# Down of a feed-forward: three of eight quads (two of six at the end) as seven products, with the weight sums by a load and an accumulating load

## The chip, the core and the metric

The kernel runs on one core of a Trainium2 chip. The metric is the device time of one execution in microseconds (us); shown is the median of three runs. TensorE (PE in the profile) multiplies, VectorE (DVE) and ScalarE (ACT) work element by element, GpSimd (POOL) does a little arithmetic and issues some DMAs, SyncE (SP) issues the loads of the weights.

## The reference

Two layers of a streaming encoder over 256 tokens of width 2048, all in float32. Layer 0 has a gated and pooled mixer, layer 1 a latent attention; each is followed by a feed-forward with 5632 hidden channels, where the change is:

```python
def swiglu(h, w_gate, w_up, w_down):
    return (jax.nn.silu(h @ w_gate) * (h @ w_up)) @ w_down
...
        x = x + mix
        x = x + swiglu(rmsnorm(x, g_ffn[layer]), w_gate[layer], w_up[layer], w_down[layer])
```

## The kernel before

Every float32 product is made of three faster ones: both factors are split into a high part (fp32r) and the rest, and TensorE multiplies high by high, high by rest, rest by high (`token_product`, lines 211 to 213, one matmul of 128x512 each). Activations are split once. Weights are split as they arrive: ScalarE copies the high part (wh, line 105), VectorE subtracts it (wl, line 106). There are six buffers of 1024 columns for each of wh and wl.

The feed-forward (`feed_forward`) goes through the hidden channels in three parts of 4, 4 and 3 groups of 512. A part first makes its hidden channels (gate and up, one call of `quads` per group), and then multiplies them by their rows of w_down, which adds to the trunk x ("Down"). Down of a part of four is two blocks, each one call of `quads` with eight quads for two blocks of 512 output columns; Down of the last part is one block of six quads, and its other 1024 output columns follow as plain token-major products with w_e.

A quad is a square of two by two tiles: two token halves, two k tiles of activations (x11, x21, x12, x22), two k tiles times two column blocks of weights (b11, b12, b21, b22; one load of 1 MB). Done plainly it is eight products, which add to the four PSUM banks c11, c12, c21, c22. Those are the four buffers of the pool ps_mm ("mm" in the profile), and the next call of `quads` gets the same four banks in the same order. In some quads the eight products are made as seven, from sums of activations and sums of weights (`quad_seven`, `quads`); four of these products add to p1, p6, p5, p7, the four banks of ps_sm ("sm"), which are combined with c once the last such quad is through. In Down `between` does that: after the last quad of seven ScalarE copies p6, and eight VectorE instructions add p1, p5, p7 and the copy to x. After the whole block four more VectorE adds bring c11, c21, c12, c22 to x (`evict`, line 316, recorded at line 253). Only then can the next call of `quads` write to these banks.

Which quads are made as seven is set by hand: `SEVEN` for gate and up, `SEVEN_DOWN` for Down, there by the number of groups in the part. The sums of activations that quads of seven need are made in `split_pair` when the hidden channels are transposed, and kept in `hforms`.

Two of the four sums of weights, t1 = b11 + b12 and t3 = b12 + b22, are one add over 1024 columns. Either VectorE adds them (`quad_seven` without t13, into the tile sums), or the loads do: GpSimd loads 1024 columns to a tile t13 (two buffers; "t" in the profile) and then a second time with an accumulating DMA (`sums_of`, lines 573 and 574). The second load waits for the first to land. Before, only the gate/up quads in `SUMMED` use loads.

The order on each engine is that of the recorded program after a scheduler has moved instructions; engines wait for each other by semaphores, each goes through its own row in order. The weights of up to three quads are asked for ahead (`AHEAD`), as far as buffers allow.

Of the kernel before, what the change touches and what calls it, by code (L numbers as in the profile page):

```python
# [8 lines left out]
F32 = mybir.dt.float32  # L9
F32R = mybir.dt.float32r  # L10
AF = mybir.ActivationFunctionType
ALU = mybir.AluOpType
AX = mybir.AxisListType

P = 128
# [7 lines left out]
SEVEN = (3, 5, 6, 7)  # L23
SUMMED = (3, 6, 7)

SEVEN_DOWN = {4: (3, 5), 3: (3,)}
AHEAD = 2
EPS = 1e-6
NH = 16
# [6 lines left out]
def trunk(ctx: ExitStack, tc: tile.TileContext, a: dict, out: bass.AP):  # L36
    nc = tc.nc
# [11 lines left out]
    def stage(**bufs):  # L49

        st = ExitStack()
        return st, *(st.enter_context(tc.tile_pool(name=n, bufs=b)) for n, b in bufs.items())

    def ev(shape, dtype=F32):

        return evs.tile([P, *shape], dtype, name="ev")
# [11 lines left out]
    at = 0  # L68
# [30 lines left out]
    def split_raw(raw, n, step=SPLIT):  # L99
        parts = []  # L100
        for o in range(0, n, step):
            m = min(step, n - o)
            wh = whs.tile([P, SPLIT], F32R, name="wh")
            wl = wls.tile([P, SPLIT], F32R, name="wl")
            nc.scalar.activation(out=wh[:, :m], in_=raw[:, o:o + m], func=AF.Copy)  # L105
            nc.vector.tensor_tensor(out=wl[:, :m], in0=raw[:, o:o + m], in1=wh[:, :m].bitcast(F32), op=ALU.subtract)  # L106
            parts.append((wh, wl, m))
        return parts
# [271 lines left out]
    def hidden():  # L380
        return big.tile([P, KD, 2 * T], F32R, name="hid")
# [8 lines left out]
    def token_sums():  # L390
        return stat.tile([P, 2, 4], F32, name="tsum")
# [8 lines left out]
    for k0 in range(0, KD, 2):  # L400
        raw = raws.tile([P, 2 * SPLIT], F32, name="raw")
        if k0 <= 2:

            n = 512 if k0 == 0 else 1024
# [52 lines left out]
    st, att, qpool = stage(att=1, qpool=2)  # L457
# [46 lines left out]
    for m in range(8):  # L504
# [10 lines left out]
        u = ev([T])  # L515
# [5 lines left out]
        for t in range(2):  # L521
            nc.vector.scalar_tensor_tensor(out=y[:, t * P:(t + 1) * P], in0=mix[:, t * P:(t + 1) * P], scalar=gain("v", m),
                                           in1=wb[:, 1, :], op0=ALU.mult, op1=ALU.add)
# [26 lines left out]
    def quad_eight(raw):  # L550
        parts = split_raw(raw, 2048)
        return dict(zip(("b11", "b12", "b22", "b21"), (block(parts, i) for i in range(4))))

    def chunks_of(layer, early):

        wgu, wd, we = (a[f"{n}{layer}"] for n in ("w_gu", "w_d", "w_e"))
        quad = lambda j, seven: "seven" if j in seven else "eight"
        todo = []
        at = 0
        for n in PARTS:  # L560
            for c in range(at, at + n):
                todo += [(wgu[c, j], "summed" if j in SUMMED else quad(j, SEVEN)) for j in range(KD // 2)]
            last = at + n == sum(PARTS)
            for b in range(1 if last else 2):
                todo += [(wd[b, 2 * at + j], quad(j, SEVEN_DOWN[n])) for j in range(2 * n)]
            if last:
                todo += [(we[c, :, i * 512:(i + 4) * 512], "whole") for c in range(2) for i in range(0, 4 * n, 4)]
            at += n

        def sums_of(src):  # L570

            t13 = early.tile([P, 1024], F32, name="t13")
            nc.gpsimd.dma_start(out=t13, in_=src[:, :1024])  # L573
            nc.gpsimd.dma_start(out=t13, in_=src[:, 512:1536], accum_op=ALU.add)
            return t13

        def load(src, kind, t13):
            raw = raws.tile([P, 2 * SPLIT], F32, name="raw")
            nc.sync.dma_start(out=raw, in_=src)
            if kind == "whole":  # L580
                return split_raw(raw, 2 * SPLIT)
            return quad_eight(raw) if kind == "eight" else quad_seven(raw, t13)

        count, begun, ready = len(todo), [], []
        for n in range(count):
            while len(ready) <= AHEAD and (todo or begun):
                while todo and len(begun) < 3:
                    src, kind = todo.pop(0)
                    begun.append((src, kind, sums_of(src) if kind == "summed" else None))
                ready.append(load(*begun.pop(0)))  # L590
            yield ready.pop(0)
# [45 lines left out]
    def feed_forward(layer, sums, scaled, g_next):  # L637
        f = None
        after = token_sums()
        at = 0  # L640
        st, hds, early = stage(hds=2, early=2)
        chunks = chunks_of(layer, early)
        for part, n in enumerate(PARTS):
            hid = hidden()
            seven_d = SEVEN_DOWN[n]
            final = part == len(PARTS) - 1

            hforms = hds.tile([P, 2, 2, 3, P] if not final else [P, 1, 2, 4, P], F32R, name="hforms", bufs=1)
            for c in range(n):
                e22 = []  # L650
                cs, (p1, p6, p5, p7) = quads(KD // 2, SEVEN, xs, scaled["forms"], chunks,
                                             lambda j, cs, ps: e22.append(copy(cs[3])) if j == KD // 2 - 2 else None)
                if f is None:
                    f = stat.tile([P, 2], F32, name="factor")
                    nc.vector.tensor_tensor(out=f, in0=trunk_rstd(sums), in1=scaled["back"], op=ALU.mult)
                e22, = e22
                e11, e12, e21, u2 = *(copy(p) for p in cs[:3]), copy(p6)
                add(e11, p1, e11)
                add(u2, p1, u2)
                add(e12, p5, e12)  # L660
                sub(e12, e12, u2)
                add(u2, p7, u2)
                add(e21, u2, e21)
                add(e22, p5, e22)
                sub(e22, e22, u2)
                hd = []
                for t, (g, u) in enumerate(((e11, e12), (e21, e22))):
                    nc.scalar.activation(out=g, in_=g, func=AF.Silu, scale=f[:, t:t + 1])
                    h = hds.tile([P, 512], F32, name="hd")
                    nc.vector.scalar_tensor_tensor(out=h, in0=u, scalar=f[:, t:t + 1], in1=g, op0=ALU.mult, op1=ALU.mult)  # L670
                    hd.append(h)
                for m in (0, 2):
                    def put(pt, hid=hid, hforms=hforms, seven_d=seven_d, m=4 * c + m):
                        pair = hid[:, m:m + 2, :]
                        src = pt.rearrange("p (j t) -> p j t", j=2)
                        if m // 2 in seven_d:
                            hg = ev([2, T])
                            nc.scalar.activation(out=hg, in_=src, func=AF.Copy)
                            split_pair(pair, hg, hforms[:, seven_d.index(m // 2)])
                        else:  # L680
                            split_pair(pair, src)
                    pending.append(lambda m=m, hd=hd, put=put: turned(lambda t, j: hd[t][:, (m + j) * P:(m + j + 1) * P], put))

            def pair_into(c, evict, hid=hid, hforms=hforms, seven_d=seven_d):
                s0, s1 = slice(c * 512, (c + 1) * 512), slice((c + 1) * 512, (c + 2) * 512)

                def between(j, cs, ps):
                    if j != seven_d[-1]:
                        return
                    if final and g_next == "final":  # L690
                        nonlocal gfin
                        gfin = big.tile([P, D], F32, name="sums")
                        nc.scalar.dma_start(out=gfin, in_=a["g_final"].broadcast_to([P, D]))
                    p1, p6, p5, p7 = ps
                    u2 = copy(p6)
                    add(x[:, 0, s0], p1, x[:, 0, s0])
                    add(u2, p1, u2)
                    add(x[:, 0, s1], p5, x[:, 0, s1])
                    sub(x[:, 0, s1], x[:, 0, s1], u2)
                    add(u2, p7, u2)  # L700
                    add(x[:, 1, s0], x[:, 1, s0], u2)
                    add(x[:, 1, s1], p5, x[:, 1, s1])
                    sub(x[:, 1, s1], x[:, 1, s1], u2)

                (c11, c12, c21, c22), _ = quads(2 * n, seven_d, hid, hforms, chunks, between)
                evict(c, (c11, c21))
                evict(c + 1, (c12, c22))

            into_trunk(None, 0, 4 * n, hid, g_next if final else None, after, chunks, pairs=range(1 if final else 2), pair_into=pair_into)
            at += n  # L710
        st.close()
        return after

    sums = feed_forward(0, sums, scaled, "mix1")

    def rotated(s):
# [12 lines left out]
    st, att, qpool = stage(att=1, qpool=2)  # L729
# [22 lines left out]
    u, y = rotated(s)  # L752
# [73 lines left out]
    for p in range(10):  # L826
# [4 lines left out]
        for i in range(3):  # L831
            if p < 8:
# [3 lines left out]
                else:  # L836
                    s = ev([T])
                    nc.vector.tensor_tensor(out=s, in0=ps, in1=rqs, op=ALU.mult)
                    u, y = rotated(s)
# [108 lines left out]
```

## Time and profile before

| | us |
|---|---|
| median of three runs (1904.33 to 1907.59) | 1904.38 |
| the profiled execution | 1904.91 |
| its span, first to last instruction | 1903.1 |
| busy: TensorE, VectorE, ScalarE, GpSimd | 1890.4, 1584.0, 1149.7, 103.9 |
| mean granted clock of TensorE, share of full speed | 0.999 |

A matmul is shown from its own start to its modelled end, and the next one starts before that; the pace is read from the starts. An instruction's time is shown with an idle time before it and what ended this idle time, where there was one.

### The profile page before, as it was taken

What the parts mean: (1) busy time and instruction counts of PE and PEld (TensorE: products, weight loads), DVE (VectorE), ACT (ScalarE), POOL (GpSimd) and SP (SyncE); (2) the same over time, 40 slices, a digit from 0 to 9 for tenths busy, and PEclk for the clock granted to TensorE, in tenths of its full rate; (3) what the DMA queues carried; (4) which work ended last, traced back from release to release, by engine and by line L of the source; (5) the groups of instructions that cost most, each with busy time, mean ns of one, the idle gap of its engine ahead of it and who ended that gap; (6) DMA issues with size and microseconds to landing.
All of it is one profiled execution on the core that took longest, in us unless ns stands there. A gap on an engine that the chain in (4) does not pass through costs nothing. (4 is left out here: it accounts for less than half of the span.)

```text
span 1903.1 us, 24047 instructions
## 1 busy us (share of the span) xinstructions
PE 1890.4 (99%) x8994; PEld 1586.9 (83%) x8994; DVE 1584.0 (83%) x2067; ACT 1149.7 (60%) x1538; POOL 103.9 (5%) x159
## 2 busy tenths in 40 slices
PE   9999999999999999999999999999999999999998
PEld 8888888888888888888889988888888888888886
DVE  7785589998799987999675755899987999978995
ACT  6554676664567654666555755776655667546663
POOL 0000001000011100000000000000100011001000
PEclk9999999999999999999999999999999999999999
DMA  8567568885688865786455255588866888757863
GB/s 310 200 219 240 183 209 291 274 266 208 215 275 274 293 235 192 251 277 237 177 180 182 93 173 194 191 278 285 262 223 208 261 289 269 255 201 254 264 238 127
DMA packets 74277, 440.19 MB, mean 231 GB/s; under 512 B 8496, under 2 KB 10288, under 8 KB 30256
## 3 DMA queue, kind: packets, MB, share of 16 engines
q1 hardware_dynamic: 53136, 364.93, 52.8%
q0 software_dynamic: 19008, 69.21, 15.4%
q10 hardware_dynamic: 2016, 4.51, 0.7%
q8 instruction: 70, 1.15, 0.2%
q14 instruction: 47, 0.39, 0.1%
HBM read 436.52 MB, written 2.10 MB: 230 GB/s over the span
## 5 line engine op out<-in xcount | busy, mean ns | idle before, releaser
L105 ACT ACTIVATE wh<-raw 128x1024 fp32r<-128x1024 f32 (+1 forms) x692 | 669.6, 986 | 470.2 <-PE mm L213 312.3
L106 DVE TENSOR_TENSOR wl<-raw,wh 128x1024 fp32r<-128x1024 f32 (+1 forms) x692 | 772.4, 1133 | 165.8 <-ACT wh L105 163.6
L211 PE MATMUL mm<-wh,xs 128*128 128x512 f32 x880 | 344.0, 391 | 0.7 <-ACT ev L252 0.7
L212 PE MATMUL mm<-wl,xs 128*128 128x512 f32 x880 | 342.5, 389 | 0.0
L213 PE MATMUL mm<-wh,xs 128*128 128x512 f32 x880 | 342.2, 389 | 0.0
L211 PE MATMUL mm<-wh,hid 128*128 128x512 f32 x852 | 333.3, 391 | 0.4 <-ACT ev L252 0.3
L213 PE MATMUL mm<-wh,hid 128*128 128x512 f32 x852 | 332.0, 390 | 0.0
L212 PE MATMUL mm<-wl,hid 128*128 128x512 f32 x852 | 331.7, 389 | 0.0
L105 ACT ACTIVATE wh<-sums 128x1024 fp32r<-128x1024 f32 x146 | 154.8, 1060 | 102.1 <-DVE sums L253 58.4
L106 DVE TENSOR_TENSOR wl<-sums,wh 128x1024 fp32r<-128x1024 f32 x146 | 177.8, 1221 | 28.6 <-ACT wh L105 24.8
L211 PEld LDWEIGHTS mm<-wh,xs 128*128 128x128 f32 x880 | 165.2, 188 | 35.0 <-ACT ev L252 1.2
L213 PEld LDWEIGHTS mm<-wh,xs 128*128 128x128 f32 x880 | 165.2, 188 | 34.3
L212 PEld LDWEIGHTS mm<-wl,xs 128*128 128x128 f32 x880 | 165.3, 188 | 33.6
L211 PEld LDWEIGHTS mm<-wh,hid 128*128 128x128 f32 x852 | 160.0, 188 | 33.7 <-ACT ev L252 0.8
L213 PEld LDWEIGHTS mm<-wh,hid 128*128 128x128 f32 x852 | 160.0, 188 | 33.2
L212 PEld LDWEIGHTS mm<-wl,hid 128*128 128x128 f32 x852 | 160.1, 188 | 32.5
L135 PE MATMUL mm<-xs,wh 128*128 128x512 f32 x375 | 133.8, 399 | 0.0
L106 DVE TENSOR_TENSOR wl<-t,wh 128x1024 fp32r<-128x1024 f32 x66 | 80.6, 1222 | 36.2 <-ACT wh L105 36.2
L136 PE MATMUL mm<-xs,wl 128*128 128x256 f32 x375 | 104.8, 280 | 0.0
L105 ACT ACTIVATE wh<-t 128x1024 fp32r<-128x1024 f32 x66 | 70.0, 1060 | 35.6 <-PE mm L213 29.8
L253 DVE TENSOR_TENSOR ev<-sm,ev 128x512 f32<-128x512 f32 x130 | 83.4, 682 | 2.4 <-ACT ev L252 2.4
L573 POOL DMA_DIRECT2D t<-in_w_gu x66 | 38.9, 590 | 835.2 <-DVE wl L106 718.0
(237 smaller groups left out, 2649.4 us busy)
## 6 DMA issues: line engine op xcount, KB each, us to landing
raw<-in_w_gu SPq DMA_DIRECT2D x176, 1024.0 KB, 5.9
raw<-in_w_d SPq DMA_DIRECT2D x76, 1024.0 KB, 4.9
t<-in_w_gu POOLq DMA_DIRECT2D x132, 512.0 KB, 6.8
raw<-in_w_o SPq DMA_DIRECT2D x32, 1024.0 KB, 4.9
raw<-in_w_e SPq DMA_DIRECT2D x12, 1024.0 KB, 4.9
raw<-in_w_v SPq DMA_DIRECT2D x10, 1024.0 KB, 6.6
raw<-in_w_z SPq DMA_DIRECT2D x8, 1024.0 KB, 4.9
raw<-in_w_u SPq DMA_DIRECT2D x8, 1024.0 KB, 4.9
```

The lines of the kernel that those rows point to most:

```text
L105: nc.scalar.activation(out=wh[:, :m], in_=raw[:, o:o + m], func=AF.Copy)
L106: nc.vector.tensor_tensor(out=wl[:, :m], in0=raw[:, o:o + m], in1=wh[:, :m].bitcast(F32), op=ALU.subtract)
L135: nc.tensor.matmul(ps, lhsT=wh, rhs=mv, start=first, stop=False)
L136: nc.tensor.matmul(ps[:, :T], lhsT=wl, rhs=mv[:, :T], start=False, stop=last)
L211: nc.tensor.matmul(ps, lhsT=hi, rhs=wh, start=first, stop=False)
L212: nc.tensor.matmul(ps, lhsT=hi, rhs=wl, start=False, stop=False)
L213: nc.tensor.matmul(ps, lhsT=lo, rhs=wh, start=False, stop=last)
L253: add = lambda out, p, q: nc.vector.tensor_tensor(out=out, in0=p, in1=q, op=ALU.add)
L573: nc.gpsimd.dma_start(out=t13, in_=src[:, :1024])
```

## The change

Quads of seven in Down: 3, 5 and 6 of eight instead of 3 and 5, and 3 and 4 of six instead of 3. All of them now take t1 and t3 from `sums_of`. `hforms` grows, and the product of gate and up is written over the up half, instead of to a tile of its own.

```diff
-SEVEN_DOWN = {4: (3, 5), 3: (3,)}
+SEVEN_DOWN = {4: (3, 5, 6), 3: (3, 4)}
...
-                todo += [(wd[b, 2 * at + j], quad(j, SEVEN_DOWN[n])) for j in range(2 * n)]
+                todo += [(wd[b, 2 * at + j], "summed" if j in SEVEN_DOWN[n] else "eight") for j in range(2 * n)]
...
-        st, hds, early = stage(hds=2, early=2)
+        st, hds, early = stage(hds=1, early=2)
...
-            hforms = hds.tile([P, 2, 2, 3, P] if not final else [P, 1, 2, 4, P], F32R, name="hforms", bufs=1)
+            hforms = hds.tile([P, len(seven_d), 2, 4 if final else 3, P], F32R, name="hforms")
...
-                    h = hds.tile([P, 512], F32, name="hd")
-                    nc.vector.scalar_tensor_tensor(out=h, in0=u, scalar=f[:, t:t + 1], in1=g, op0=ALU.mult, op1=ALU.mult)
-                    hd.append(h)
+                    nc.vector.scalar_tensor_tensor(out=u, in0=u, scalar=f[:, t:t + 1], in1=g, op0=ALU.mult, op1=ALU.mult)
+                    hd.append(u)
```

What moves on the engines is seen in their rows. First VectorE at the end of the first Down block of layer 0, from the middle of the eight instructions of `between` on (sm_3884 is p7; mm_3727, 3729, 3728, 3730 are c11, c21, c12, c22 of this block; wl are splits of the weights of the quads to come). Before, where `between` belongs to quad 5:

```order
L254 TENSOR_TENSOR x_82<-x_82,ev_3971 128x512
L106 TENSOR_TENSOR wl_3984<-raw_3981,wh_3983 128x1024
L253 TENSOR_TENSOR ev_3971<-sm_3884,ev_3971 128x512
L106 TENSOR_TENSOR wl_3988<-raw_3981,wh_3987 128x1024
L253 TENSOR_TENSOR x_82<-x_82,ev_3971 128x512
L254 TENSOR_TENSOR x_82<-x_82,ev_3971 128x512
L106 TENSOR_TENSOR wl_4018<-raw_4015,wh_4017 128x1024
L106 TENSOR_TENSOR wl_4022<-raw_4015,wh_4021 128x1024
L253 TENSOR_TENSOR x_82<-mm_3727,x_82 128x512
L253 TENSOR_TENSOR x_82<-mm_3729,x_82 128x512
L253 TENSOR_TENSOR x_82<-mm_3728,x_82 128x512
L253 TENSOR_TENSOR x_82<-mm_3730,x_82 128x512
```

And in the changed kernel, where `between` belongs to quad 6 (sm_3892 is p7; mm_3722, 3724, 3723, 3725 are c11, c21, c12, c22):

```order
L254 TENSOR_TENSOR x_82<-x_82,ev_4021 128x512
L106 TENSOR_TENSOR wl_4037<-raw_4034,wh_4036 128x1024
L253 TENSOR_TENSOR ev_4021<-sm_3892,ev_4021 128x512
L106 TENSOR_TENSOR wl_4041<-raw_4034,wh_4040 128x1024
L253 TENSOR_TENSOR x_82<-x_82,ev_4021 128x512
L254 TENSOR_TENSOR x_82<-x_82,ev_4021 128x512
L253 TENSOR_TENSOR x_82<-mm_3722,x_82 128x512
L253 TENSOR_TENSOR x_82<-mm_3724,x_82 128x512
L253 TENSOR_TENSOR x_82<-mm_3723,x_82 128x512
L253 TENSOR_TENSOR x_82<-mm_3725,x_82 128x512
L106 TENSOR_TENSOR wl_4079<-raw_4076,wh_4078 128x1024
L106 TENSOR_TENSOR wl_4083<-raw_4076,wh_4082 128x1024
```

The eight instructions of `between` come one quad later, and the two splits that stood between them and the four adds of c now stand behind these adds. The ends of the eight blocks of parts of four and of the last part's block in layer 0 read like this, nine in all.

Second, GpSimd from the last gate/up quad of the first part on. Before, the loads of the next part's gate/up quads follow:

```order
L573 DMA t13_3504<-in_w_gu0 128x1024
L574 DMA t13_3504<-in_w_gu0 128x1024
L573 DMA t13_4327<-in_w_gu0 128x1024
L574 DMA t13_4327<-in_w_gu0 128x1024
L573 DMA t13_4453<-in_w_gu0 128x1024
```

In the changed kernel the loads for six Down quads (3, 5, 6 of both blocks) stand between, here down to the second block's first:

```order
L573 DMA t13_3498<-in_w_gu0 128x1024
L574 DMA t13_3498<-in_w_gu0 128x1024
L573 DMA t13_3668<-in_w_d0 128x1024
L574 DMA t13_3668<-in_w_d0 128x1024
L573 DMA t13_3760<-in_w_d0 128x1024
L574 DMA t13_3760<-in_w_d0 128x1024
L573 DMA t13_3831<-in_w_d0 128x1024
L574 DMA t13_3831<-in_w_d0 128x1024
L573 DMA t13_4031<-in_w_d0 128x1024
L574 DMA t13_4031<-in_w_d0 128x1024
```

With two buffers, quad 6's tile (t13_3831) is the one that quad 3's (t13_3668) leaves free.

Third, VectorE at the end of the last part's Down block in layer 1, where each eviction is followed by a multiplication by the final gain (line 324). Before, from the middle of `between` on (mm_15925, 15927, 15926 are c11, c21, c12):

```order
L254 TENSOR_TENSOR x_82<-x_82,ev_16094 128x512
L106 TENSOR_TENSOR wl_16107<-raw_16104,wh_16106 128x1024
L253 TENSOR_TENSOR ev_16094<-sm_16070,ev_16094 128x512
L106 TENSOR_TENSOR wl_16111<-raw_16104,wh_16110 128x1024
L253 TENSOR_TENSOR x_82<-x_82,ev_16094 128x512
L254 TENSOR_TENSOR x_82<-x_82,ev_16094 128x512
L106 TENSOR_TENSOR wl_16141<-raw_16138,wh_16140 128x1024
L106 TENSOR_TENSOR wl_16145<-raw_16138,wh_16144 128x1024
L253 TENSOR_TENSOR x_82<-mm_15925,x_82 128x512
L253 TENSOR_TENSOR x_82<-mm_15927,x_82 128x512
L253 TENSOR_TENSOR x_82<-mm_15926,x_82 128x512
```

In the changed kernel (mm_16062, 16064, 16063 are c11, c21, c12; two splits and the first steps of `between` stand ahead of these rows):

```order
L253 TENSOR_TENSOR ev_16284<-sm_16226,ev_16284 128x512
L106 TENSOR_TENSOR wl_16297<-raw_16294,wh_16296 128x1024
L254 TENSOR_TENSOR x_82<-x_82,ev_16284 128x512
L106 TENSOR_TENSOR wl_16301<-raw_16294,wh_16300 128x1024
L253 TENSOR_TENSOR ev_16284<-sm_16229,ev_16284 128x512
L253 TENSOR_TENSOR x_82<-mm_16062,x_82 128x512
L253 TENSOR_TENSOR x_82<-x_82,ev_16284 128x512
L254 TENSOR_TENSOR x_82<-x_82,ev_16284 128x512
L253 TENSOR_TENSOR x_82<-mm_16064,x_82 128x512
L324 TENSOR_TENSOR x_82<-x_82,sums_16282 128x512
L253 TENSOR_TENSOR x_82<-mm_16063,x_82 128x512
```

Here c11's add stands ahead of the last two instructions of `between`, and a multiplication by the gain ahead of c12's.

## Rows read from the trace of the kernel before

**Rows 1.** Busy time of TensorE on the page: us, share of the span, instructions.

```profile
PE 1890.4 (99%) x8994; PEld 1586.9 (83%) x8994; DVE 1584.0 (83%) x2067; ACT 1149.7 (60%) x1538; POOL 103.9 (5%) x159
```

**Rows 2.** Waits of TensorE, the longest: us in total, times, longest.

```profile
PE mm L211 <- ACT ev L252: 1.1, 2, 0.7
```

**Rows 3.** Windows: PE, PEld, DVE, ACT, POOL busy; clock, DMA share, GB/s.

```profile
408.23:451.28 43.05, 43.05 (x195) 35.74 (x194) 40.86 (x50) 23.72 (x28) 0.85 (x1) 1.00 0.74 252
451.28:493.40 42.12, 42.12 (x187) 34.90 (x186) 34.52 (x39) 20.49 (x22) 0.00 (x0) 1.00 0.56 200
366.50:408.23 41.73, 41.73 (x189) 34.61 (x188) 40.24 (x51) 28.14 (x36) 4.22 (x6) 1.00 0.88 278
```

**Rows 4.** Timeline of TensorE, quad 5's end and the next block's start: start, duration.

```profile
440.18 0.39 PE L213 MATMUL sm<-wh,hforms 128*128 128x512 f32 x1
440.40 0.39 PE L211 MATMUL mm<-wh,hid 128*128 128x512 f32 x1
...
451.28 0.39 PE L211 MATMUL mm<-wh,hid 128*128 128x512 f32 x1
...
451.96 0.39 PE L211 MATMUL mm<-wh,hid 128*128 128x512 f32 x1
```

**Rows 5.** Timeline of VectorE in the same stretch.

```profile
438.14 0.68 DVE L253 TENSOR_TENSOR x<-sm,x 128x512 f32<-128x512 f32 x1
438.74 2.35 DVE L106 TENSOR_TENSOR wl<-raw,wh 128x1024 fp32r<-128x1024 f32 x2
441.01 0.68 DVE L253 TENSOR_TENSOR x<-sm,x 128x512 f32<-128x512 f32 x1
441.61 0.68 DVE L253 TENSOR_TENSOR ev<-sm,ev 128x512 f32<-128x512 f32 x1
...
446.87 0.69 DVE L254 TENSOR_TENSOR x<-x,ev 128x512 f32<-128x512 f32 x1
447.48 2.35 DVE L106 TENSOR_TENSOR wl<-raw,wh 128x1024 fp32r<-128x1024 f32 x2
449.75 2.48 DVE L253 TENSOR_TENSOR x<-mm,x 128x512 f32<-128x512 f32 x4
```

**Rows 6.** Timeline of ScalarE, the copy of p6.

```profile
440.60 0.60 ACT L252 ACTIVATE ev<-sm 128x512 f32<-128x512 f32 x1 [0.29 <-PE sm L213]
```

**Rows 7.** Timeline, layer 1, end of the last Down block: VectorE and TensorE.

```profile
1860.95 1.88 DVE L253 TENSOR_TENSOR x<-mm,x 128x512 f32<-128x512 f32 x3
...
1861.29 0.39 PE L213 MATMUL mm<-wh,hid 128*128 128x512 f32 x1
...
1861.78 0.47 PE L211 MATMUL mm<-wh,hid 128*128 128x512 f32 x1
...
1862.09 0.39 PE L212 MATMUL mm<-wl,hid 128*128 128x512 f32 x1
```

**Rows 8.** Timeline, the same block: VectorE behind p1 and p5; quad 3's end.

```profile
1849.40 3.49 DVE L106 TENSOR_TENSOR wl<-raw,wh 128x1024 fp32r<-128x1024 f32 x3
...
1850.63 0.39 PE L211 MATMUL mm<-wh,hid 128*128 128x512 f32 x1
```

**Rows 9.** Groups by line and shape: busy us, mean ns of one, idle before.

```profile
L253 DVE TENSOR_TENSOR sums<-raw 128x1024 f32<-128x1024 f32 x40 | 48.9, 1222 | 3.9 <-DMA raw<-in_w_gu 3.6
...
L275 DVE TENSOR_TENSOR ev<-ev 128x128 f32<-128x128 f32 x18 | 5.1, 286 | 0.1
```

**Rows 10.** Timeline of GpSimd: the loads that meet the pair before them.

```profile
403.39 0.87 POOL L573 DMA_DIRECT2D t<-in_w_gu  x1
414.08 0.85 POOL L574 DMA_DIRECT2D t<-in_w_gu  x1 [9.82 <-DMA t<-in_w_gu]
```

**Rows 11.** Lines 573 and 574, from issue to landing.

```profile
DMA to landing us min/median/max: 3.9/5.8/11.6
...
DMA to landing us min/median/max: 5.4/7.6/13.1
```

**Rows 12.** Timeline of VectorE, first Down block: quad 3's sums.

```profile
417.25 1.22 DVE L253 TENSOR_TENSOR sums<-raw 128x1024 f32<-128x1024 f32 x1
...
421.32 1.22 DVE L106 TENSOR_TENSOR wl<-sums,wh 128x1024 fp32r<-128x1024 f32 x1
```

## Prediction

> **What bounds the kernel now.** I read the busy shares first: TensorE is busy for 99% of the span [rows 1]. A busy share alone doesn't prove a bound, so the next view is TensorE's list of waits: its longest entry adds up to 1.1 us over the whole run [rows 2]. Then the windows: one from the start of a part's first Down block to its end, the second block, and the gate/up column group ahead of them. TensorE has no idle time in any of the three, at a granted clock of 1.00 (2.4 GHz), while VectorE is busy for 40.9 of 43.1 us, 34.5 of 42.1 and 40.2 of 41.7, and the DMA share is highest, 0.88, in gate/up [rows 3]. So TensorE sets the pace, and VectorE is close behind. Last the timeline, for the pace itself: one matmul of 512 columns starts 0.226 us after the one before, although it is shown with 0.39 us [rows 4]; over the 48 matmuls of the two quads from 440.40 to 451.28 it is 10.88 / 48 = 0.2267 us [rows 4]. I use 0.2267. Three matmuls (one product) take 0.68 us, a quad of eight products 24 x 0.2267 = 5.44 us, one of seven 4.76 us.
>
> **What is removed from TensorE.** Each layer runs two Down blocks in each of two parts of four and one in the part of three, so five blocks, and each gets one more quad of seven. That is 10 quads, each three matmuls shorter: 30 x 0.2267 = 6.8 us. Nothing else of TensorE's work changes.
> The row says 0.2267 us for one such matmul. The Trainium skill, "TensorE: Matmul & The Clock Gate", section "Back-to-back issue gap", gives about 131 ns for 512 columns in a sustained stream; by that the 30 matmuls would be an estimated 3.9 us, and my end result 2.9 us higher. The row doesn't agree with it, and the row decides.
>
> **What moves between VectorE and the loads.** A quad that now has its two sums loaded loses the add of 1024 columns, 1.22 us [rows 9]. A quad that becomes one of seven gains three things on VectorE: 1536 more columns to split (a split of 1024 at 1.22 us [rows 12], one of 512 at the 0.68 us of the 512-column adds in [rows 5]) and two adds of 512 (0.68 each). Per block of eight quads: minus 2 x 1.22, plus 1.22 + 0.68 + 2 x 0.68 = 3.26, so 0.8 us more. The first block of a part also makes one more set of sums of the activations: four subtractions of 128 columns at 0.286 us [rows 9] and a split of 384 columns, below 0.68 us; ScalarE gets two more copies, each at most the 0.60 us of a 512-column one [rows 6]. On this total VectorE stays below TensorE: 34.5 + 0.8 of 41.4 us in a second block; in a first one the durations add up to 40.9 + 2.6 = 43.5 of 42.4, but neighbours overlap (they start 0.60 us apart at a duration of 0.68 [rows 5]), over the 50 instructions [rows 3] by 4 us. I cost this at nothing: the cover is the three quads of lead that the splits have. Without cover the price is at most those 0.8 to 2.6 us a block. The product that was written to a tile of its own and is now written over the up half has the same size, and costs nothing.
>
> **What is moved to the end of the block: the term that decides.** The four ps_sm sums p1, p6, p5, p7 can be taken out only when the last quad of seven is through. Before, that is quad 5, with quads 6 and 7 behind it (10.88 us); now it is quad 6, with only quad 7 behind it (5.44 us). I call E the moment at which the last quad of seven ends on TensorE. In the block shown E = 440.40 and the next block begins at 451.28 [rows 4]. ScalarE copies p6 at E + 0.20 to E + 0.80 [rows 6]. VectorE, without idle time, takes p1, makes two splits, is at p5 at E + 0.61 and at the last of the eight instructions at 446.87; at 447.48, E + 7.08, it is through with them [rows 5]. Two more splits follow, then the four adds that empty c11, c21, c12, c22, from 449.75, 0.60 us apart [rows 5]. The first, c11's, ends at 449.75 + 0.68 = 450.43, which is 0.85 us ahead of 451.28, where the next block's first product writes the same bank. The third, c12's, ends at 451.63, 0.33 us ahead of 451.96, where c12's bank is written again [rows 4]. So it fits today, with little to spare.
> In the changed order VectorE's row from E on is the same up to the last of the eight (the splits in between are those of the next two quads, as before), and the four adds follow at once. Then c11's add starts at E + 7.08 and ends at E + 7.76, and c12's ends at E + 8.96. The next block is due at E + 5.44, and c12's product at E + 6.12. c11 is 2.32 us late, c12 2.84 us. How TensorE starts again is seen once in the rows: the add that begins at 1860.95 frees c11's bank at 1861.63, the matmul starts at 1861.78, 0.15 us later, and the one after it 0.31 us behind, 0.08 more than the usual pace [rows 7]. So c12's product starts at E + 9.11 instead of E + 6.12, 2.99 us late, and 0.08 is lost in starting: **3.07 us a block end**. c21 and c22 are out in time by then. Queued behind TensorE's wait is all the rest of the kernel, and nobody gives the time back, since TensorE is never behind on anything else.
> Nine of the ten block ends have this order (in layer 0 the last one leads into the plain token-major blocks, which use c11's and c12's banks in the same turn). The tenth is the end of layer 1. There E is 1850.63, and VectorE was through with p1 and p5 at 1849.40, E - 1.23 [rows 8]. Two splits at 1.14 us (two take 2.27 us in [rows 5]) bring it to E + 1.04; in the new order six steps (0.60, 1.14, 0.60, 1.14, 0.60 and then c11) put c11's add at E + 5.12, and after four more of 0.60 before it c12's starts at E + 8.12 and ends at 8.80. With 0.15 and 0.08, against 6.12, that is 2.9 us; the block end loses 1861.78 - 1861.52 + 0.08 = 0.34 us already [rows 7], so 2.6 are new.
> Bounds for this price, from both sides: if all four splits were done before E, VectorE would start at E + 0.80 with p6's copy, and seven adds of 0.60 and c11's 0.68 end at E + 5.68, c12's at 6.88, so that c12 is 0.99 us late with its start: 1.0 us a block end at least, as the eight instructions themselves don't fit into 5.44 us. Upwards it grows by whatever VectorE is late at E; I take 3.07, since the splits stand between in the order and the rows show them there.
>
> **The sum.** Profiled execution 1904.9; - 6.8 + 9 x 3.07 + 2.6 = + 23.4, so 1928.3; the median shown is 0.5 us lower than the profiled run: **1927.8 us**, 1.2% slower. Less than 0.2% (3.8 us) can hardly be told from no change here.
>
> **Rivals.**
> 1. The sums come out in time and the gain stays: 1904.4 - 6.8 = 1897.6, faster. It needs c11's bank free within 5.44 us of E, that is, four splits and one of the eight instructions moved out of the way. For it speaks that the evictions fit today; against it that the margin is 0.85 us, while quad 6's 5.44 us go and only two splits (2.27 us) are taken out from between. Chance 0.05.
> 2. The block ends cost less, 1.0 to 2.2 us, because VectorE has some of the splits behind it: 1904.4 - 6.8 + 10 to 22 = 1908 to 1920. Chance 0.08, of which 0.04 end within 0.2% of before.
> 3. The loads of quad 6's sums come late on top. There are two buffers for them, so quad 6's first load waits for quad 3's split. In the first block that split begins at 421.32 today and one add (1.13 us) earlier after the change, so it ends at 421.4 [rows 12]. First load 5.8 us, 0.3 to the next issue, accumulating load 7.6 (medians) [rows 11]: 435.1. VectorE needs them at 438.0, because two adds of 0.60 and a split of 1.22 must be done at 440.40, when quad 6 begins. With a load that meets other traffic, as the pair from 403.39, issued again at 414.08 [rows 10] and landed 7.6 later, it is 439.7: 1.7 us late. In four first blocks that is 7 us: 1935. With the longest of each, 11.6 and 13.1 [rows 11], it would be 8.4 us a block. Chance 0.12.
>
> The forecast itself has the remaining 0.75, with 1921 to 1933 as its own range (0.7 us either way at each block end). The range given reaches from rival 2's upper part to rival 3: 1917 to 1937. Slower by over 0.2%: 0.75 + 0.12 + 0.04 = 0.91; within: 0.04; faster: 0.05.
>
> **What the profile after would show.** Right: ten gaps of TensorE in Down, at each block's end, some 2.4 us before the first product and some 0.5 before the second, each ended by a VectorE add of x from an mm bank; 30 fewer matmuls at the old pace; no gap elsewhere. Wrong: the four adds early enough and no gap (rival 1), shorter gaps with splits ahead of p1 (rival 2), or a gap in front of quad 6 of a first block, with VectorE waiting for a load (rival 3). What would make all of this wrong is a VectorE that, at the last quad of seven, runs further ahead or further behind than in [rows 5].

## The result and the profile after

The changed kernel takes 1951.31 us (median of four runs, 1943.11 to 1963.08) against 1904.68 us before (four runs, 1904.33 to 1907.59): a ratio of 1.0244, interval 1.0223 to 1.0265. The forecast was 1927.8 with a range of 1917 to 1937. The direction was right; the loss is twice the forecast one. The profiled execution is the longest of the four, with a span of 1961.3 us against 1903.1.

The page first: busy times, then TensorE's granted clock in 40 slices (one 8 where all were 9).

```profile
PE 1906.1 (97%) x8964; PEld 1594.0 (81%) x8964; DVE 1603.5 (82%) x2119; ACT 1168.1 (60%) x1570; POOL 142.9 (7%) x215
...
PEclk9999999998999999999999999999999999999999
```

Against [rows 1] there are the 30 matmuls fewer that were expected, yet TensorE is busy for longer. Its list of waits (us in total, times, longest), where [rows 2] had 1.1 us at the top:

```profile
PE mm L211 <- DVE x L253: 31.1, 9, 5.9
PE mm L212 <- DVE wl L106: 9.0, 3, 3.7
PE mm L211 <- ACT wh L105: 2.3, 1, 2.3
```

The first and third lines are the block ends; the second is a wait that the forecast's sum did not contain (its rival 3 did). Windows: the first Down block up to the restart behind it, the second one in the same way (both had no idle time in [rows 3]), and two stretches behind a wait. Columns as in [rows 3].

```profile
408.23:460.23 52.00, 44.49 (x193) 36.12 (x192) 42.27 (x56) 27.59 (x33) 5.06 (x7) 0.94 0.86 272
460.23:506.25 46.02, 43.73 (x183) 35.73 (x184) 35.66 (x41) 21.99 (x23) 4.20 (x6) 0.95 0.74 239
442.96:447.40 4.44, 4.44 (x12) 3.49 (x13) 4.44 (x5) 3.88 (x4) 0.55 (x1) 0.62 0.85 172
460.79:465.50 4.71, 4.71 (x15) 3.70 (x14) 3.35 (x4) 0.27 (x1) 0.00 (x0) 0.61 0.48 165
```

So there are three losses, and the rows below take them one by one. A wait is counted from start to start of two matmuls, less the pace of 0.2267 us.

**The end of a second block** is as forecast, less one step. TensorE, then VectorE (start, duration, in brackets idle time and what ended it):

```profile
503.57 0.39 PE L213 MATMUL mm<-wh,hid 128*128 128x512 f32 x1
506.25 0.47 PE L211 MATMUL mm<-wh,xs 128*128 128x512 f32 x1 [2.30 <-ACT wh L105]
...
507.02 0.40 PE L211 MATMUL mm<-wh,xs 128*128 128x512 f32 x1
...
499.56 0.68 DVE L253 TENSOR_TENSOR ev<-sm,ev 128x512 f32<-128x512 f32 x1
...
504.83 0.68 DVE L254 TENSOR_TENSOR x<-x,ev 128x512 f32<-128x512 f32 x1
505.43 2.47 DVE L253 TENSOR_TENSOR x<-mm,x 128x512 f32<-128x512 f32 x4
```

Quad 6 ended at 498.36 (E). The four adds begin at 505.43, E + 7.07, where E + 7.08 was forecast; the first ends at 506.11, and TensorE restarts at 506.25, 0.14 later. The wait is 506.25 - 503.57 - 0.23 = 2.45 us. The bracket names ScalarE, but the splits of this quad's weights, which come after that copy, were through by 504.30; the add of 505.43 is what came 0.14 ahead. Then the second bank is written at 507.02, while the third add runs to 507.31: the matmul did not wait for it, only for the first two (the second ends at 506.71). The banks that the changed program assigns say why: behind these blocks the next c12 lies in the bank that c21 had, and the next c21 in that of c12. All four second blocks show 2.46 us.

**In front of quad 6 of a first block** a load is late. GpSimd, VectorE and TensorE:

```profile
422.55 0.55 POOL L573 DMA_DIRECT2D t<-in_w_d  x1 [6.67 <-DVE ev L274]
429.82 0.85 POOL L574 DMA_DIRECT2D t<-in_w_d  x1 [6.72 <-DMA t<-in_w_d]
...
421.03 1.22 DVE L106 TENSOR_TENSOR wl<-t,wh 128x1024 fp32r<-128x1024 f32 x1
...
440.35 0.69 DVE L253 TENSOR_TENSOR sums<-t,raw 128x512 f32<-128x512 f32 x1 [7.00 <-issue]
...
440.48 0.39 PE L211 MATMUL mm<-wh,hid 128*128 128x512 f32 x1
442.96 0.50 PE L212 MATMUL mm<-wl,hid 128*128 128x512 f32 x1 [2.09 <-DVE wl L106]
```

Quad 3's split of its t13 ends at 422.25, the load for quad 6 is issued at 422.55, its accumulating half at 429.82, and the sums are usable at 440.35, 17.8 us after the first issue. VectorE stood for 7.00 us. TensorE waits 2.25 us here, 3.30 and 3.90 in layer 1's two first blocks, and not at all in the second part of layer 0.

**The end of the same block** comes later still. SyncE's load of weights, ScalarE, VectorE, TensorE:

```profile
443.53 0.33 SPq L579 DMA_DIRECT2D raw<-in_w_d  x1
...
451.94 1.06 ACT L105 ACTIVATE wh<-raw 128x1024 fp32r<-128x1024 f32 x1 [4.95 <-DMA raw<-in_w_d]
452.91 0.58 ACT L252 ACTIVATE ev<-sm 128x512 f32<-128x512 f32 x1
...
459.40 2.48 DVE L253 TENSOR_TENSOR x<-mm,x 128x512 f32<-128x512 f32 x4
...
454.43 0.39 PE L213 MATMUL mm<-wh,hid 128*128 128x512 f32 x1
460.23 0.76 PE L211 MATMUL mm<-wh,hid 128*128 128x512 f32 x1 [5.41 <-DVE x L253]
```

The raw buffer that VectorE's late work held is asked for again at 443.53 (before, the load at this place was issued at 438.25). This load also takes longer, 8.3 us to its landing against 5.1, while GpSimd's loads of sums run (one issued at 441.81, the next at 444.94). ScalarE waits for that load until 451.94, and the copy of p6 stands behind it in ScalarE's row: 452.91 is E + 3.7 (E = 449.21), against E + 0.20 in [rows 6]. The four adds begin at E + 10.2, and TensorE waits 460.23 - 454.43 - 0.23 = 5.57 us. The four first blocks wait 5.58, 3.41, 6.08 and 4.61 us, and the last block of layer 0, the ninth of the ends that the forecast priced alike, 4.03 us.

**The clock.** Behind nine of these waits matmuls start 0.427 us apart instead of 0.2267, 7 to 13 of them: the granted clock is at its lower level (1.2 GHz) there, which makes the means of the two windows above 0.62 and 0.61. Over the run 91 matmuls are so (7 of them at the program's start), 0.2 us each, 17.8 us. The sum: waits 47.8 us (2.3 before) and clock 17.8 (0.2 before), less 6.8 for the matmuls, is + 56.3 of the + 58.2 between the two spans.

### The profile page after: what moved, and what is told of

Same layout as the page of the kernel before. It is cut to its first block, busy times and chain, and to the rows that moved or that the text cites. A ratio compares the mean times of both kernels' runs of the same rounds, so it can differ in the third digit from the quotient of the medians.

```text
span 1961.3 us, 24181 instructions
## 1 busy us (share of the span) xinstructions
PE 1906.1 (97%) x8964; PEld 1594.0 (81%) x8964; DVE 1603.5 (82%) x2119; ACT 1168.1 (60%) x1570; POOL 142.9 (7%) x215
## 5 line engine op out<-in xcount | busy, mean ns | idle before, releaser
L211 PE MATMUL mm<-wh,hid 128*128 128x512 f32 x792 | 315.9, 399 | 24.3 <-DVE x L253 24.2
L212 PE MATMUL mm<-wl,hid 128*128 128x512 f32 x792 | 313.5, 396 | 9.0 <-DVE wl L106 9.0
L213 PE MATMUL mm<-wh,hid 128*128 128x512 f32 x792 | 313.0, 395 | 0.0
L211 PEld LDWEIGHTS mm<-wh,hid 128*128 128x128 f32 x792 | 151.9, 192 | 58.2 <-issue 21.2
L105 ACT ACTIVATE wh<-sums 128x1024 fp32r<-128x1024 f32 x138 | 146.0, 1058 | 76.2 <-DVE sums L253 44.7
L212 PEld LDWEIGHTS mm<-wl,hid 128*128 128x128 f32 x792 | 151.9, 192 | 41.1 <-DVE wl L106 10.2
L106 DVE TENSOR_TENSOR wl<-sums,wh 128x1024 fp32r<-128x1024 f32 x138 | 167.9, 1220 | 20.0 <-ACT wh L105 16.9
L213 PEld LDWEIGHTS mm<-wh,hid 128*128 128x128 f32 x792 | 151.6, 191 | 32.0
L106 DVE TENSOR_TENSOR wl<-t,wh 128x1024 fp32r<-128x1024 f32 x94 | 114.7, 1221 | 46.8 <-ACT wh L105 46.8
L105 ACT ACTIVATE wh<-t 128x1024 fp32r<-128x1024 f32 x94 | 99.6, 1059 | 66.2 <-PE mm L213 40.8
L253 DVE TENSOR_TENSOR sums<-t,raw 128x512 f32<-128x512 f32 x94 | 64.6, 687 | 27.7 <-issue 26.6
```

Source lines behind the costliest of these rows:

```text
L211: nc.tensor.matmul(ps, lhsT=hi, rhs=wh, start=first, stop=False)
L212: nc.tensor.matmul(ps, lhsT=hi, rhs=wl, start=False, stop=False)
L213: nc.tensor.matmul(ps, lhsT=lo, rhs=wh, start=False, stop=last)
L253: add = lambda out, p, q: nc.vector.tensor_tensor(out=out, in0=p, in1=q, op=ALU.add)
```

## The experiments

Three theories were on record. **A**: the block ends are too short for the sums of the quads of seven, wherever the sums of weights come from, and the clock falls behind the wait. **B**: the late loads are the cause (two t13 buffers). **C**: VectorE has no room for the third quad of seven. Each run stands beside runs of the kernel before on the same chip (medians 1904.46 to 1905.13).

**All sums by VectorE** (no loads in Down, three quads of seven):

```diff
-  ... "summed" if j in SEVEN_DOWN[n] else "eight" ...
+  ... quad(j, SEVEN_DOWN[n]) ...
```

> The changed quads, but VectorE makes all sums of Down's weights itself, no loads for them. Theory A (the sums of the seven-quads leave too late at each block's end, and the clock falls behind that wait): ten waits for c11 of about 2.5 us stay, none in front of quad 6; 1904.7 - 6.8 + 25 + some 10 us of halved clock = about 1932. Theory B (the late loads with two buffers are the cause, the block ends only follow from them): the excess goes with the loads, 1898 to 1905. Theory C (VectorE has no room for a third quad of seven): waits for weights all over Down, over 1940.

Measured: 1947.03, ratio 1.0219 (1.0203 to 1.0235), in C's range, but without the waits for weights all over Down that C named. The second blocks wait 2.47 us each, so these ends do not need the loads (A). The waits in front of quad 6 are gone but for 0.5 us (B). But the first blocks wait 5.06 to 5.34 us without any late load. ScalarE and VectorE in the first one, where E = 446.18 and the next block is due at 451.88:

```profile
448.41 0.58 ACT L252 ACTIVATE ev<-sm 128x512 f32<-128x512 f32 x1
...
444.78 4.62 DVE L106 TENSOR_TENSOR wl<-raw,wh 128x1024 fp32r<-128x1024 f32 x4
449.32 0.69 DVE L253 TENSOR_TENSOR x<-sm,x 128x512 f32<-128x512 f32 x1
...
450.52 1.28 DVE L253 TENSOR_TENSOR x<-sm,x 128x512 f32<-128x512 f32 x2
...
456.38 2.48 DVE L253 TENSOR_TENSOR x<-mm,x 128x512 f32<-128x512 f32 x4
```

With four splits back to back ahead of them, VectorE comes to p1 at E + 3.1 and to p5 at E + 4.3, which it had at E + 0.61 in [rows 5], and its four adds begin at E + 10.2 instead of E + 7.07. So with three adds of 1024 columns in the block it is behind, with no load of sums in the block (C, for this kernel).

**Loads alone** (`SEVEN_DOWN = {4: (3, 5), 3: (3,)}` as before, all else as changed):

> The quads of before (3 and 5 of eight, 3 of six) with the sums of t1 and t3 by loads. A: nothing moves at the block ends, 1904 to 1905, no waits of TensorE. B: with two tiles per block each load has at least eight quads, and is in time: 1904 to 1905 too. If accumulating loads as such slow the other loads down, waits for raw weights appear and it is over 1908.

Measured: 1904.49, ratio 0.9999 (0.9986 to 1.0011). Loading the sums, growing tiles and the rewritten product cost nothing by themselves; it takes the third quad of seven.

**The four c evictions ahead of `between`** in parts of four:

```diff
-  ... = quads(2 * n, seven_d, hid, hforms, chunks, between)
+  ..., ps = quads(2 * n, seven_d, hid, hforms, chunks, between if final else lambda j, cs, ps: None)
...
+  if not final:
+      between(seven_d[-1], None, ps)
```

> The changed kernel, but in the blocks of the parts of four VectorE brings c11, c21, c12, c22 to x first, and the sums of the seven-quads after them. A: eight of the ten waits at block ends go (only the two last parts keep theirs, some 6 us with the clock); the waits in front of quad 6 of the first blocks stay, some 9 us and 5 of clock: about 1918. B: the block ends were late by the loads, so little changes: 1940 to 1950.

Measured: 1918.97, ratio 1.0067 (1.0047 to 1.0087), A's time (about 1918), though not A's parts: it had all eight ends gone and some 9 us left in front of quad 6. The waits of the second blocks are gone, which leaves waits in first blocks (4.37 and 2.97 us at two ends, 1.04 and 1.94 in front of quad 6) and at the last ones (2.9 and 1.26). The order at the block's end is one cause, not the only one.

**Quads of seven at 2, 3, 5** (2, 3 of six), so that two plain quads follow as before; sums of 3 and 5 loaded, of 2 by VectorE:

> As many quads of seven, but at 2, 3, 5 of eight and 2, 3 of six, so that two plain quads stand behind the last; loads for 3 and 5, VectorE's own sums for 2. A: the evictions fit again and the loads are early enough: the 6.8 us are gained, 1898, no waits. B: the same, as no tile is needed three quads after it came free. C: VectorE is the bound, 1905 or more, with waits for weights.

Measured: 1922.85, ratio 1.0089 (1.0065 to 1.0113), where A and B had 1898: a miss. Second blocks end without a wait of more than 0.31 us; first ones still wait 2.2 to 3.1 us at three of four ends. ScalarE in the first block, where the last quad of seven ends at 442.14:

```profile
444.20 1.06 ACT L105 ACTIVATE wh<-raw 128x1024 fp32r<-128x1024 f32 x1 [3.20 <-DMA raw<-in_w_d]
445.16 0.58 ACT L252 ACTIVATE ev<-sm 128x512 f32<-128x512 f32 x1
```

Again the copy of p6 stands behind a split that waits for a raw load. This load was issued at 435.28, 4.0 us later than the same one in the kernel before (431.28), and took 8.8 us instead of 4.9, so a slow load had a part in it beside a late one.

**Mixed sums**: quad 3 of eight by VectorE's add, 5 and 6 loaded:

```diff
-  ... "summed" if j in SEVEN_DOWN[n] else "eight" ...
+  ... ("seven" if n == 4 and j == 3 else "summed") if j in SEVEN_DOWN[n] else "eight" ...
```

> The changed kernel, but the sums of quad 3 of eight are made by VectorE's own add (as in the kernel before), and only those of quads 5 and 6 (and of 3 and 4 of six) are loaded, so that with two buffers no load has to wait for a quad that is computed directly before it. Theory A (the end of a block is 2.46 us too short for its sums, wherever they come from, and the clock falls behind it): about 1945 to 1950 us, as e1. Theory B (the late loads are the cause, in front of quad 6 and at the ends of the first blocks): no wait in front of quad 6, all first-block ends fall to the 2.46 us of the second blocks, 1925 to 1932 us. Theory C (VectorE has no room in the first blocks): no wait in front of quad 6, but first-block ends stay at 4 to 5 us since VectorE has one add of 1.22 us more in each block than with loads: 1938 to 1948 us.

Measured: 1928.39, ratio 1.0122 (1.0109 to 1.0136), in B's range. VectorE has more to do than in the changed kernel, and still there is no wait in front of quad 6, and all eight ends of blocks of eight wait 2.46 or 2.47 us, first and second alike. This is 23 us off the changed kernel, with C's load on VectorE increased. TensorE's waits, the load of raw weights, and the windows of the first block and of 3.4 us behind it:

```profile
PE mm L211 <- DVE x L253: 20.9, 9, 2.5
...
437.99 0.33 SPq L579 DMA_DIRECT2D raw<-in_w_d  x1
...
408.23:453.86 45.63, 43.33 (x196) 35.68 (x195) 44.27 (x58) 28.43 (x34) 3.64 (x5) 1.00 0.86 282
...
454.18:457.58 3.40, 3.40 (x10) 2.64 (x9) 3.40 (x5) 0.00 (x0) 0.00 (x0) 0.52 0.83 322
```

The raw load is issued at 437.99 again. The clock still falls behind five of the ten block ends, 1.2 to 1.6 us each: behind the four first blocks (2.46 us) and the last block of layer 0 (2.67 us), and behind none of the four second blocks (2.46 us too).

**A third t13 buffer**, all else as changed (early=3; one ev tile less makes room), and its control, the changed kernel with six ev tiles:

> The changed kernel with a third buffer for the loaded sums t13 (room for it is made by one ev tile less, six in place of seven), so that the loads of quad 6's sums need not wait until quad 3's are used; the data moved is the same. Theory B (it is the wait of quad 6's loads for a buffer that makes quad 6 and the first-block ends late): the waits in front of quad 6 go and the first-block ends fall to 2.46 us, as in e5: 1926 to 1932 us. Rival (it is the extra data, 469.6 MB against 440.2, that makes the raw loads land late): landings of raw stay near 6.9 us, the first-block ends stay at 3.4 to 6.1 us, 1940 to 1955 us. What the missing ev tile costs by itself is read from e10.

> The changed kernel with six ev tiles in place of seven and two buffers of t13 as it has: the control for e9. If an ev tile less costs nothing: 1945 to 1955 us, as the changed kernel. If evictions and token work wait for it: longer than 1955.

Measured: 1931.83 (ratio 1.0128, 1.0104 to 1.0151) and 1944.61 (1.0214, 1.0174 to 1.0255). The kernel with three buffers, GpSimd's two loads for the first quad 6 and TensorE's waits:

```profile
405.69 0.88 POOL L573 DMA_DIRECT2D t<-in_w_d  x1
413.66 0.85 POOL L574 DMA_DIRECT2D t<-in_w_d  x1 [7.09 <-DMA t<-in_w_d]
...
PE mm L211 <- DVE x L253: 20.9, 9, 2.9
```

The load is issued at 405.69, 16.9 us earlier than in the changed kernel, no matmul waits in front of quad 6, and the first blocks' ends wait 2.46, 2.46, 2.46 and 2.74 us. The rival, extra data, falls for these ends: as much is moved, and raw loads of w_d take 7.3 us in the median (6.9 in the changed kernel, 4.9 before), without harm to them. So the late load, the one thing in which the kernel differs from its control, is the cause of both the wait in front of quad 6 and the longer ends. The control shows on which way: its first block waits only 0.7 us in front of quad 6 and still 8.3 us at its end, with the raw load issued at 441.72 and landed 9.4 us later, ScalarE's split at 451.27 and the copy of p6 at 452.23. It is the raw load, and not TensorE's own wait, that carries the delay to the end. Some of what the third buffer leaves is new: five waits for ScalarE's copies to ev tiles, 5.6 us together (1.8 us in the control).

**Filled waits**: the kernel of the first experiment with 161 products of a zero weight tile behind the blocks:

```diff
+  zero = const.tile([P, P], F32R, name="zero")
...
+  fill = (21 if layer == 0 else 0) if final else 24 if c == 0 else 11
...
+  for i in range(fill):
+      nc.tensor.matmul(c22, lhsT=zero, rhs=xs[:, 0, :], start=False, stop=i == fill - 1)
```

> e1_own_sums with 24 products of a zero weight tile behind each first block of a part of four, 11 behind each second block and 21 behind the last block of layer 0, added into the last bank, so that TensorE works through the waits of e1 (each product 0.2267 us: 5.4, 2.5 and 4.8 us) and changes no value. It tells what the lower granted clock behind the waits costs: if the 9 us that e1 lost in stretches of 0.427 us products come from TensorE having stood still, they go: 1935 to 1940 us against e1's 1947, and the granted clock of the blocks after is as it was before. If the clock falls for another reason, or the products only lengthen the ends, the time stays at 1945 to 1952.

Measured: 1937.95, ratio 1.0172 (1.0158 to 1.0185), 9.1 us less than without the filling, which is the 9.0 us that the first experiment's trace shows in 46 matmuls at the lower level. The window behind the first block without the filling, then, with it, TensorE through the former wait and the window of the whole block with it:

```profile
457.54:461.50 3.96, 3.96 (x10) 3.10 (x10) 3.96 (x6) 0.00 (x0) 0.00 (x0) 0.50 0.45 188
```

```profile
452.03 5.75 PE L710 MATMUL mm<-xs,zero 128*128 128x512 f32 x24
457.62 0.39 PE L214 MATMUL mm<-wh,hid 128*128 128x512 f32 x1
...
408.23:456.80 48.57, 48.57 (x219) 40.17 (x219) 47.27 (x60) 28.85 (x35) 0.85 (x1) 1.00 0.68 233
```

The end is no shorter (the next block starts at 457.62, without the filling at 457.22) and nothing else was sped up, so standing still is what costs the clock: 0.50 behind a wait, 1.00 where TensorE worked through it.

**Fewer splits**: the kernel of the first experiment, with four splits less for VectorE at the start of each first block of a part of four (`quad_high`: wh stands in for wl, so the low halves of these weights are left out of the product):

> e1_own_sums, but the first two quads of the first block of each part of four take the high halves of their weights for the low halves too (the low halves of these two quads are left out of the product), so that VectorE has four splits of about 1.15 us less to make at the start of each first block; TensorE's products are the same in number. Theory C (VectorE arrives late at the end of the first block): the first-block ends fall from e1's 5.1 to 5.3 us to the 2.47 us of the second blocks and little clock is lost behind them, about 1930 to 1935 us against e1's 1947. If VectorE's fullness is not what makes the first blocks' ends longer, they stay at 5 us and the time stays within 2 us of e1.

Measured: 1945.01, ratio 1.0211 (1.0195 to 1.0227): a miss in the time. The waits at three of the four first ends fell to 2.46 us and the first to 3.94, as C had it, but a new wait took the gain. TensorE's waits, and VectorE at the first of these places:

```profile
PE sm L262 <- DVE ev L679: 9.5, 5, 2.7
...
413.95 1.23 DVE L253 TENSOR_TENSOR sums<-raw 128x1024 f32<-128x1024 f32 x1 [3.91 <-DMA raw<-in_w_d]
415.09 0.69 DVE L254 TENSOR_TENSOR ev<-ev 128x512 f32<-128x512 f32 x1
```

With the splits gone, quad 3's add moved ahead in VectorE's row and waits 3.91 us for its weights, with the work of gate and up queued behind it, for which the transposes (L262) wait. TensorE stands there for 2.05, 2.10, 2.78 and 2.53 us in the four blocks, which also gives VectorE that much more time up to the end. Both waits together are 5.99, 4.56, 5.24 and 5.00 us, against 5.34, 5.06, 5.32 and 5.09 at the ends in the first experiment: the wait has moved rather than gone, and this run does not show what VectorE's fullness costs.

**Both mended**: mixed sums, late `between`, and the part of three with one quad of seven as before:

```diff
-SEVEN_DOWN = {4: (3, 5, 6), 3: (3, 4)}
+SEVEN_DOWN = {4: (3, 5, 6), 3: (3,)}
...
```

> The seven-quads of a part of four as in e5_mixed_sums (3 by VectorE's add, 5 and 6 loaded), the part of three as in the kernel before with its one quad's sums loaded, and in parts of four the four evictions of the c banks ahead of those of the sums of seven-quads. 24 products fewer than before (8 x 3), 5.4 us. If A and B name all that is lost (block ends and late loads), no wait is left: about 1899 us, faster than the kernel before. If C holds too, first blocks keep waits of 1 to 4 us and some clock: 1905 to 1918.

Measured: 1898.42, ratio 0.9964 (0.9952 to 0.9977), faster than the kernel before, and what was expected if A and B name all that is lost. 24 matmuls fewer make 5.4 us; 6.0 were gained. Its page and the window of its first Down block:

```profile
PE 1884.5 (99%) x8970; PEld 1582.2 (83%) x8970; DVE 1603.7 (85%) x2109; ACT 1163.1 (61%) x1562; POOL 129.2 (7%) x195
...
408.23:450.56 42.33, 42.33 (x193) 35.15 (x191) 40.75 (x53) 26.29 (x32) 3.66 (x5) 1.00 0.85 289
```

VectorE is as busy as in the changed kernel (1603.7 against 1603.5 us), and TensorE has no idle time in the block.

## Why the prediction was too low

- **Matmuls removed:** right, 30 fewer, 6.8 us. Both the pace and the count hold.
- **The block ends, "3.07 us a block end":** the mechanism and its first half were right to 0.01 us (adds at E + 7.07, c11 2.32 late, restart 0.14 later). The failed step is "c12's product starts at E + 9.11 ... 2.99 us late": it took the next group's second bank for the one that the third add empties. The banks are handed on in the order in which they came free (c11, c21, c12, c22), so the next c12 gets the bank of c21, which the second add empties; that the next call gets the same four banks in the same order, as the section on the kernel before has it, is not so. The end costs 2.46, not 3.07; in the kernel with mixed sums, where eight of the nine show it and the ninth waits 2.67, they were priced 5.3 us too dear.
- **The last end of layer 1:** forecast 2.6 us new beside the 0.34 of before, measured 1.49 in all (1.64 with mixed sums).
- **The clock:** no term of the sum stood for it. With ends of 2.46 us alone (mixed sums) it costs 6.9 us beyond the start of the program. So the forecast of 1927.8 and the measured 1928.39 of that kernel agree by luck, because errors cancel: 5.3 too much at nine ends and 1.3 at the last, 6.9 missing for the clock. The filled waits show that the standing is the cause. The Trainium skill, "TensorE: Matmul & The Clock Gate", section "A second HAM failure mode: psum-queue depth-cycling", describes this: short idle times between groups of matmuls, while PSUM banks are cycled, make the clock go back and forth between its levels, and the throughput pays. The trace agrees: 0.50 to 0.62 in the windows behind the waits.
- **The late load of quad 6's sums, which the sum had at nothing and left to rival 3:** this is the step that made the forecast wrong. The rival named the mechanism and the place (two t13 buffers, quad 6's load behind quad 3's split), but priced it by the wait in front of quad 6 alone, "1.7 us late", 7 us in all, at a chance of 0.12. That price was not far off: the sums were usable at 440.35, where its dearer case had 439.7, and the waits were 9.45 us in all. What was not followed is what the late load holds up: VectorE's row stands 7 us, so "the three quads of lead that the splits have", by which the forecast put VectorE's extra work at nothing, are used up; the raw buffer comes free 5.3 us later, its load lands 8.5 us later, ScalarE's split waits for it, and the copy of p6 stands behind that split. This made the four first ends 9.8 us longer together than 4 x 2.46, and the longer waits took 10.3 us more of clock (17.8 against 7.5). Together that is 29.6 of the 33.4 us between the spans of the changed kernel and of the one with mixed sums; in medians it is 22.9, as the profiled execution is the longest of its four.
- **VectorE's room (C):** it is real, but not what decided here: with one more add than the changed kernel (mixed sums) the ends were 2.46 us; with three more (all by VectorE) the first ends were 5.1 to 5.3. These two kernels differ only in who adds for quads 5 and 6 of a part of four (and for the part of three), VectorE or the loads, so it is VectorE's adds that lengthen the first ends there.
- **Rivals 1 and 2:** neither came. The second blocks' 2.46 us is between rival 2's 2.2 and the forecast's 3.07; for the gain to stay, as in rival 1, `between` has to give way, which the kernel with both mends shows.

"Perfetto Trace Analysis" of the Trainium skill, section "Matmuls", says in other words what the block ends show: groups of matmuls should go round different PSUM banks, so that emptying one overlaps the next group. This kernel has eight buffers, four for c and four for p, and the next block writes c again, so it waited until the first of them was emptied, 2.46 us in the rows; putting c first made it fit. The trace agrees with the rule in that.

What stays open: why the clock falls behind some waits of 2.46 us and not behind others. In the changed kernel it fell behind two of the four second blocks (762.2 and 1492.5, not 503.6 and 1759.2), with mixed sums behind all four first blocks and no second one. Open too is why the changed kernel's time varies by 20 us from run to run; the account above is that of the longest run.

## What to carry over

When work is taken from the bounding engine, look at what then stands last in front of each buffer that it writes next: a gain of 0.68 us a quad was lost more than three times over at a block end where the banks came free 2.46 us late. Price a late load not by the wait that it causes directly but by every row that it stands in: which buffers its consumer holds, which loads those hold up, and which short instruction (here a copy of 0.58 us) is queued behind them. And count a wait of the bounding engine at more than its length where the granted clock falls behind it.

## What the runs showed of the hardware

Behind a wait of TensorE the granted clock can go to its lower level: 0.50 in the first experiment's window from 457.54 to 461.50, where matmuls of 512 columns start 0.427 us apart against 0.2267. Each such stretch of 6 to 13 matmuls costs 1.2 to 2.5 us; behind a wait of 2.46 us that was 1.2 to 1.6, so the wait cost half as much again. A load and an accumulating load of 512 KB each, one behind the other, took 17.8 us from the first issue to the first use where raw loads ran beside them (422.55 to 440.35 in the changed kernel, from 429.82 on for the second alone).
